# Rotating a matrix by 90 degrees: filling both PSUM tiles row tile by row tile in the first output of a macro tile

## The chip, the cores and the metric

The kernel runs on one core of one Trainium2 chip. Times are device microseconds (us) of one execution. A profile comes from one of these executions; its span runs from the first to the last instruction and is about 2 us shorter than the time (1266.0 us of 1267.77 in the kernel before).

In this kernel SP issues the loads, DVE reverses rows, PE transposes blocks of 128 by 128 into tiles in PSUM (`pt` in the profile's lines), ACT copies from there into an output buffer and issues the stores, and 16 DMA engines move the data. A DMA share of 1.0 means that all 16 are busy. PE's clock is given as a share of its full speed; the records show 1.00 and 0.50 (in the kernel before, 0.50 from 1214 to 1216.5 us and 1.00 from 1221.5 to 1222.5 us), and a mean in between where it turns.

## The reference

```python
def setup_inputs():
    return {
        "x": np.random.randn(8192, 8192).astype(np.float32),
        "k": 1,
    }

def reference(x, k):
    return np.rot90(x, k)
```

A counter-clockwise turn by 90 degrees is a reversal of each row followed by a transpose. The matrix has 268 MB, and each byte is read once and written once.

## The kernel before

The matrix is cut into macro tiles of 1024 rows by 4096 columns. Each has eight row tiles of 128 rows, and each row tile is one load of 2 MB. There are 15 full macro tiles. The sixteenth is cut into two half-height ones of four row tiles each, and both are loaded before either is put out.

```python
def load(r0, rt, c0):                       # rt = 8, or 4 for a half-height macro tile
    for t in range(rt):
        a = a_pool.tile([P, W], dt, tag="a")                  # 2 buffers
        nc.sync.dma_start(out=a[:], in_=x[r0 + t*P : r0 + (t+1)*P, c0 : c0 + W])
        for j in range(W // CH):
            ar = r_pool.tile([P, CH // P, P], dt, tag="ar")   # 68 buffers
            nc.vector.tensor_copy(out=ar[:], in_= ... [:, :, ::-1])   # reversal
            chunks[t, j] = ar
# ... cut: the first loads borrow o_pool's buffers

def store(r0, rt, c0, chunks, end):
    # full height: PW = 2, G = 4.  half height: PW = 4, G = 8
    for i, g0 in enumerate(range(0, W // P, G)):              # one output = one store of 2 MB
        ot = o_pool.tile([P, F], dt, tag="o")                 # 2 buffers (cut: at the end a_pool's too)
        for h in range(0, G, PW):                             # two PSUM tiles for each output
            pt = psum_pool.tile([P, FP], mybir.dt.float32, tag="ps")   # 2 buffers
            for w in range(PW):
                for t in range(rt):
                    nc.tensor.transpose(ps[...], chunks[t, ...], ident)   # 16 for each PSUM tile
            nc.scalar.copy(o[:, G - PW - h : G - h, :], ps)
            # after the second copy: the store, issued on ACT's queue
            ...
            nc.scalar.dma_start(out=dst, in_=...)
# ... cut
for m in most:
    store(*m, load(*m), False)
c1 = load(*before_last)
c2 = load(*last)
store(*before_last, c1, True)
store(*last, c2, True)
```

A tile framework adds all waits, and a scheduler orders the instructions of each engine. The order in the source goes tile by tile: an output's first PSUM tile gets all its 16 transposes, two for each row tile in a full-height macro tile, before the second gets any. So when the last row tile of a macro tile arrives, only 7 of the first output's 32 transposes are done.

Of the kernel before, what the change touches and what calls it, by code (L numbers as in the profile page):

```python
# [2 lines left out]

# [5 lines left out]

P = 128  # L10




R = 1024
RT = R // P
LAST = [4, 4]
W = 4096
CH = 512
F = 4096  # L20
FP = 2048


def whole_reads(nc):






    for fn in nc.m.functions:
        for block in fn.blocks:
            for n, ins in enumerate(block.instructions):
                if not isinstance(ins, mybir.InstDMACopy):
                    continue
                src = ins.ins[0]
                ap = [list(d) for d in src.ap]
                if len(ap) == 3 and ap[2][0] == 1 and ap[1][0] == ap[2][1]:
                    ap = [ap[0], [1, 1], [1, ap[1][1] * ap[2][1]]]
                    block.instructions[n] = copy.replace(  # L40
                        ins,
                        ins=[copy.replace(src, ap=ap)],
                        ant_dge_precooked=False,
                    )


def macro_tiles(N, M):

    tiles = [(r0, RT, c0) for r0 in range(0, N, R) for c0 in range(0, M, W)]
    r0, _, c0 = tiles.pop()  # L50
    for n in LAST:
        tiles.append((r0, n, c0))
        r0 += n * P
    return tiles


@with_exitstack
def kernel(
    ctx: ExitStack,
    tc: tile.TileContext,  # L60
    x: bass.AP,
    k: bass.AP,
    out: bass.AP,
):
    nc = tc.nc
    assert k == 1, f"only k=1 supported, got {k}"
    nc.at_finalize(whole_reads)

    N, M = x.shape
    dt = x.dtype  # L70

    consts = ctx.enter_context(tc.tile_pool(name="consts", bufs=1))
    ident = consts.tile([P, P], dt)
    make_identity(nc, ident)

    a_pool = ctx.enter_context(tc.tile_pool(name="a_pool", bufs=2))
    r_pool = ctx.enter_context(tc.tile_pool(name="r_pool", bufs=68))
    o_pool = ctx.enter_context(tc.tile_pool(name="o_pool", bufs=2))
    psum_pool = ctx.enter_context(
        tc.tile_pool(name="psum", bufs=2, space=bass.MemoryType.PSUM)  # L80
    )

    loads = 0

    def load(r0, rt, c0):





        nonlocal loads
        chunks = {}
        for t in range(rt):


            if loads < RT and loads % 4 >= 2:
                a = o_pool.tile([P, W], dt, tag="o")
            else:
                a = a_pool.tile([P, W], dt, tag="a")
            loads += 1  # L100
            nc.sync.dma_start(
                out=a[:], in_=x[r0 + t * P : r0 + (t + 1) * P, c0 : c0 + W]
            )
            for j in range(W // CH):
                ar = r_pool.tile([P, CH // P, P], dt, tag="ar")
                nc.vector.tensor_copy(  # L106
                    out=ar[:],
                    in_=a[:, j * CH : (j + 1) * CH].rearrange(
                        "r (b m) -> r b m", m=P
                    )[:, :, ::-1],  # L110
                )
                chunks[t, j] = ar
        return chunks

    def store(r0, rt, c0, chunks, end):





        rows = rt * P
        PW = 1
        while 2 * PW * rows <= FP:
            PW *= 2
        G = PW
        while 2 * G * rows <= F:
            G *= 2
        for i, g0 in enumerate(range(0, W // P, G)):
            if end and i % 2 == 0:
                ot = a_pool.tile([P, F], dt, tag="a")  # L130
            else:
                ot = o_pool.tile([P, F], dt, tag="o")
            o = ot[:, : G * rows].rearrange("m (g f) -> m g f", g=G)

            S = PW if end and r0 + rows == N and g0 + G == W // P else G
            for h in range(0, G, PW):
                pt = psum_pool.tile([P, FP], mybir.dt.float32, tag="ps")
                ps = pt[:, : PW * rows].rearrange("m (g f) -> m g f", g=PW)
                for w in range(PW):
                    g = g0 + h + w  # L140
                    for t in range(rt):
                        nc.tensor.transpose(  # L142
                            ps[:, PW - 1 - w, t * P : (t + 1) * P],
                            chunks[t, g * P // CH][:, g % (CH // P), :],
                            ident,
                        )
                nc.scalar.copy(o[:, G - PW - h : G - h, :], ps)  # L147

                done = h + PW
                if done % S == 0:  # L150
                    top = M - c0 - (g0 + done) * P
                    dst = out[top : top + S * P, r0 : r0 + rows].rearrange(
                        "(g m) f -> m g f", g=S
                    )
                    nc.scalar.dma_start(  # L155
                        out=dst, in_=o[:, G - done : G - done + S, :]
                    )

    tiles = macro_tiles(N, M)
    *most, before_last, last = tiles  # L160
# [9 lines that stand above are left out]
# [1 line left out]
_INS = ['x', 'k']  # L171
_OUTS = [((8192, 8192), 'float32')]

_NUMBERS = {'k': 1}


# [26 lines left out]
```

## Time and profile before

| What | Value |
| --- | --- |
| time, median of 3 runs | 1267.77 us (1267.59 to 1268.42) |
| span of the profiled run | 1266.0 us |
| PE, DVE, ACT busy | 55%, 28%, 37% |
| DMA, mean rate over the span | 425 GB/s |
| idle time of ACT before its copies | 742.6 us, of which 729.5 us wait for a store to free its buffer |
| one output on ACT | two copies of 1.87 us and the issue of the store (0.55 us) |

The way to read this is from the last row upward. ACT waits for stores most of the time (729.5 us), PE waits for ACT (465.9 us), and DVE waits for loads (811.4 us). These waits lead back, for the most part, to the DMA, whose share is 1.01, at 429 GB/s, from 70 to 980 us.

### The profile page before, as it was taken

The page shows a single profiled execution, that of the slowest core. Times are in us where ns is not written, and L with a number is a line of the kernel's source. Part 1 is how long each engine was busy: PE and PEld are TensorE (multiplying, and loading weights), DVE is VectorE, ACT ScalarE, POOL GpSimd, SP SyncE. Part 2 cuts the span into 40 slices and gives each one's busy share as a digit, 9 for nine tenths or more (in the row PEclk, how much of TensorE's full clock was granted, in tenths as well). Part 3 has the DMA queues.
Part 4 walks back from the last instruction along what each step waited for, and adds up shares of the span by engine and source line. Part 5 has one row for each costly group of instructions (what it writes and reads, how often), then busy time and mean ns, then how long its engine had stood idle before and what let it go on. Part 6 is the DMA issues. An engine that isn't in the chain of part 4 may idle for free.

```text
span 1266.0 us, 10386 instructions
## 1 busy us (share of the span) xinstructions
PE 700.4 (55%) x4096; PEld 660.8 (52%) x4096; DVE 354.9 (28%) x1024; ACT 467.3 (37%) x257; POOL 0.7 (0%) x6
## 2 busy tenths in 40 slices
PE   1456455665655555555556546565464665656573
PEld 0355455554545455554555445464464654556573
DVE  4422322232222322233222322233222332223210
ACT  0333334333433334333433334333433334333364
POOL 0000000000000000000000000000000000000000
PEclk9986777777678777787777877778777667777687
DMA  9999999999999999999999999999999999999998
GB/s 398 416 431 429 429 428 429 430 427 430 427 429 429 429 429 430 428 429 428 430 428 428 429 429 427 427 429 426 430 429 427 414 428 430 426 427 428 428 393 370
DMA packets 37057, 537.55 MB, mean 425 GB/s; under 512 B 4112, under 2 KB 4112, under 8 KB 4112
## 3 DMA queue, kind: packets, MB, share of 16 engines
q10 hardware_dynamic: 18576, 268.44, 50.0%
q1 hardware_dynamic: 18432, 268.44, 49.9%
q8 instruction: 32, 0.52, 0.2%
q14 instruction: 17, 0.14, 0.0%
HBM read 268.44 MB, written 268.44 MB: 424 GB/s over the span
## 4 chain that ended last, share of the span: by engine, by line
DMA 78%; ACT 19%; issue 1%; DVE 1%; ACTq 0%; PE 0%; DVEq 0%
DMA out_dram<-ot 74%; ACT ot L147 19%; DMA a<-in_x_dram 3%; DVE ar L106 1%; ACTq L155 0%; PE pt L142 0%; ACTq L147 0%; DVEq L106 0%
## 5 line engine op out<-in xcount | busy, mean ns | idle before, releaser
L142 PE MATMUL pt<-ident,ar 128*128 128x128 f32 x4096 | 700.4, 350 | 548.3 <-ACT ot L147 465.9
L142 PEld LDWEIGHTS pt<-ident,ar 128*128 128x128 f32 x4096 | 660.8, 187 | 587.7 <-ACT ot L147 496.4
L147 ACT COPY ot<-pt 128x2048 f32<-128x2048 f32 x256 | 466.0, 1869 | 742.6 <-DMA out_dram<-ot 729.5
L106 DVE COPY ar<-a 128x512 f32<-128x512 f32 x1024 | 354.9, 420 | 865.8 <-DMA a<-in_x_dram 811.4
L147 ACT ACT_TABLE_LOAD x1 | 1.3, 1283 | 41.1 <-DVE ar L106 41.1
masks.py:199 POOL TENSOR_SCALAR_AFFINE_SELECT ident<-ident 128x128 f32<-128x128 f32 x1 | 0.3, 294 | 0.1
masks.py:197 POOL MEMSET ident<- 128x128 f32 x1 | 0.2, 205 | 0.3 <-POOLq L184 0.3
L184 POOL MEMSET const-bfloat16-1.0<- 128x1 bf16 x1 | 0.1, 102 | 0.0
L184 POOL MEMSET const-uint8-127<- 128x1 uint8 x1 | 0.1, 102 | 0.0
L184 POOL MEMSET const-float32-0.0<- 128x1 f32 x1 | 0.1, 99 | 0.2 <-issue 0.2
L184 POOL MEMSET const-float32-1.0<- 128x1 f32 x1 | 0.1, 99 | 0.0
## 6 DMA issues: line engine op xcount, KB each, us to landing
a<-in_x_dram SPq DMA_DIRECT2D x128, 2048.0 KB, 16.8
out_dram<-ot ACTq DMA_DIRECT2D x127, 2048.0 KB, 15.9
out_dram<-ot ACTq DMA_DIRECT2D x2, 1024.0 KB, 13.7
```

The lines of the kernel that those rows point to most:

```text
L106: nc.vector.tensor_copy(out=ar[:], in_=a[:, j * CH : (j + 1) * CH].rearrange("r (b m) -> r b m", m=P)[:, :, ::-1],)
L142: nc.tensor.transpose(ps[:, PW - 1 - w, t * P : (t + 1) * P], chunks[t, g * P // CH][:, g % (CH // P), :], ident,)
L147: nc.scalar.copy(o[:, G - PW - h : G - h, :], ps)
L184: nc = _bacc.Bacc("TRN2", target_bir_lowering=False, num_devices=1)
```

## The change

The intent is to shorten what has to follow the arrival of a macro tile's last row tile. For the first output, both PSUM tiles are taken at once, and the transposes go by row tile over both of them: 28 of the 32 can be done before the last row tile has come, and four remain instead of 25.

```diff
+            ps = {}
+
+            def transposes(t, ws):
+                for w in ws:
+                    g = g0 + w
+                    nc.tensor.transpose(
+                        ps[w // PW][:, PW - 1 - w % PW, t * P : (t + 1) * P],
+                        chunks[t, g * P // CH][:, g % (CH // P), :],
+                        ident,
+                    )
+
+            def psum_tile(h):
+                pt = psum_pool.tile([P, FP], mybir.dt.float32, tag="ps")
+                ps[h] = pt[:, : PW * rows].rearrange("m (g f) -> m g f", g=PW)
+
+            if i == 0 and (rt == RT or r0 + rows < N):
+                for h in range(G // PW):
+                    psum_tile(h)
+                for t in range(rt):
+                    transposes(t, range(G))
             for h in range(0, G, PW):
-                pt = psum_pool.tile([P, FP], mybir.dt.float32, tag="ps")
-                ps = pt[:, : PW * rows].rearrange("m (g f) -> m g f", g=PW)
-                for w in range(PW):
-                    ... (16 transposes into this tile)
-                nc.scalar.copy(o[:, G - PW - h : G - h, :], ps)
+                if h // PW not in ps:
+                    psum_tile(h // PW)
+                    for w in range(h, h + PW):
+                        for t in range(rt):
+                            transposes(t, [w])
+                nc.scalar.copy(o[:, G - PW - h : G - h, :], ps[h // PW])
```

The condition takes in the 15 full macro tiles and the first of the two half-height ones.

More of the change, by code (lines that the diff above doesn't have):

```diff
@@ L135, in store @@
             S = PW if end and r0 + rows == N and g0 + G == W // P else G
-            for h in range(0, G, PW):
-                pt = psum_pool.tile([P, FP], mybir.dt.float32, tag="ps")
-                ps = pt[:, : PW * rows].rearrange("m (g f) -> m g f", g=PW)
-                for w in range(PW):
-                    g = g0 + h + w
-                    for t in range(rt):
-                        nc.tensor.transpose(
-                            ps[:, PW - 1 - w, t * P : (t + 1) * P],
-                            chunks[t, g * P // CH][:, g % (CH // P), :],
-                            ident,
-                        )
-                nc.scalar.copy(o[:, G - PW - h : G - h, :], ps)
+            ps = {}
[15 more added lines that the diff above has]
+                    transposes(t, range(G))
+            for h in range(0, G, PW):
+                if h // PW not in ps:
[4 more added lines that the diff above has]
+                nc.scalar.copy(o[:, G - PW - h : G - h, :], ps[h // PW])
                 done = h + PW
```

## The prediction

> **What bounds the kernel now.** I read the page's busy row and its slices first, then the chain that ended last, then a table of stretches, then the timeline at one macro tile boundary, then the chain through the end.
>
> ```profile
> PE 700.4 (55%) x4096; PEld 660.8 (52%) x4096; DVE 354.9 (28%) x1024; ACT 467.3 (37%) x257; POOL 0.7 (0%) x6
> ...
> DMA  9999999999999999999999999999999999999998
> ...
> DMA 78%; ACT 19%; issue 1%; DVE 1%; ACTq 0%; PE 0%; DVEq 0%
> ```
>
> No compute engine is over 55% busy, and the DMA row is full in 39 of 40 slices. In the chain that ended last, PE has 0%. The 19% of ACT in that chain lies, in the steady state, beside other transfers: a store's landing releases the two copies into its buffer, while another store and two loads are still under way. So the question is not how long the chain is but when the 16 DMA engines run dry. The table of stretches answers it; its last three columns are the granted PE clock, the DMA share and GB/s, and its first count is PE's instructions.
>
> ```profile
> 4.00:50.00 46.00, 11.14 (x46) 7.98 (x47) 24.16 (x70) 5.02 (x3) 0.00 (x0) 1.00 1.00 428
> 50.00:70.00 20.00, 11.38 (x85) 10.62 (x82) 5.79 (x18) 7.28 (x4) 0.00 (x0) 0.83 1.01 409
> 70.00:980.00 910.00, 507.69 (x2951) 480.63 (x2951) 255.65 (x738) 338.32 (x186) 0.00 (x0) 0.75 1.01 429
> ...
> 1214.00:1216.50 2.50, 2.50 (x13) 2.50 (x13) 0.00 (x0) 1.43 (x1) 0.00 (x0) 0.50 0.27 111
> 1216.50:1221.50 5.00, 4.78 (x43) 4.50 (x42) 2.78 (x8) 3.69 (x3) 0.00 (x0) 0.98 0.99 419
> 1221.50:1222.50 1.00, 1.00 (x11) 1.00 (x10) 0.00 (x0) 1.00 (x1) 0.00 (x0) 1.00 0.70 295
> ```
>
> From 4 us to 1214 us the DMA share is 1.0 throughout, at 428 to 429 GB/s but for small dips (409 at 50 to 70 us). The engines run dry in three places only: the first 4 us, 1214 to 1216.5 us (share 0.27), and the end. The second is where the loads are over and only stores remain, just as the first half-height macro tile starts to be put out. Of everything the change touches, only that place lies next to an idle DMA.
>
> [...] PE idles 3 to 6 us between outputs, the granted clock is 0.50 at many restarts, and 32 transposes take 3.7 us (warm) to 6.6 us (cold).
> [...] 32 of them took 3.74 us with the clock at 1.00 and 16 took 3.40 us at 0.50, that is 0.11 us and 0.21 us apiece. I use the trace's figures.
>
> **The change part by part.** Counts are unchanged: 4096 transposes, 1024 reversals, 256 copies, and the built programs have the same order on ACT, DVE and SP. Only the order on PE differs, in the first output of 16 of the 17 macro tiles (15 full ones and the first of two half-height ones), 32 transposes each. One copy (ACT) empties one PSUM tile (16 transposes), two copies make one store.
>
> *(a) The 14 inner boundaries.* The timeline of one:
>
> ```profile
> 583.63 1.36 PEld L142 LDWEIGHTS pt<-ident,ar 128*128 128x128 f32 x7 [4.13 <-ACT ot L147]
> ...
> 588.31 4.50 PEld L142 LDWEIGHTS pt<-ident,ar 128*128 128x128 f32 x25 [3.32 <-DVE ar L106]
> 588.31 4.74 PE L142 MATMUL pt<-ident,ar 128*128 128x128 f32 x25 [2.92 <-DVE ar L106]
> 591.49 3.63 ACT L147 COPY ot<-pt 128x2048 f32<-128x2048 f32 x2 [6.14 <-DMA out_dram<-ot]
> ```
>
> PE does 7, waits for the last row tile at 588.31, does 25 and ends at 593.05. ACT starts at 591.49, because a store's landing let it, and needs the second PSUM tile at 591.49 + 1.87 = 593.36: PE is 0.3 us early. After the change 28 transposes come before the last row tile's four. In the built program the order is 8 into the first PSUM tile, 8 into the second once its copy has ended (about 585.4), then four for each later row tile. At 0.21 us each they end near 585.4 + 24 x 0.21 = 590.4. So both tiles are full by about 590.5, 1 us before the first copy and 3 us before the second. What is removed is ACT's small stall at the boundaries where PE was late: the timeline shows four (0.27, 0.95, 0.57 and 0.50 us, 2.3 us in all). But the DMA share is 1.0 there, so a store issued half a microsecond sooner only queues longer. I count 0 for this part.
>
> *(b) The first macro tile.* Its last row tile is ready at 43.6 us, and the first copy starts at 45.83 after 9 more transposes into its tile; it will be 2 (0.4 us instead of about 1.9). So the first two stores go out some 1.5 us sooner, at about 48.1 and 52.7 instead of 49.65 and 54.16. In that time loads fill the DMA engines, so this mostly swaps loads for stores. Only the dip to 409 GB/s between 50 and 70 us (20 us x 20/429 = 0.9 us lost) could shrink. I count -0.3 us, a guess within 0 to -0.9.
>
> *(c) The half-height macro tile at the end.* All its rows were converted long before, so it has no last row tile to wait for. The chain through this place:
>
> ```profile
> 1195.80 15.92 DMA out_dram<-ot
> ...
> 1211.80 1.88 ACT ot L147
> 1213.67 0.04 issue
> 1213.72 3.40 PE pt L142 x16
> 1217.12 0.02 issue
> 1217.14 3.66 ACT ot L147 x2
> 1220.80 0.02 issue
> 1220.82 0.55 ACTq L155
> ```
>
> Here PE is on the path. It gets a free PSUM tile at 1213.67, fills it with 16 transposes by 1217.12, and only then can ACT copy. After the change the same 32 transposes are dealt out over both tiles, and the built program lets the first copy go after the 28th instead of the 16th. The whole 32 took 5.13 us here (the clock turns at about 1216.6), so the 28th ends at about 5.13 - 4 x 0.11 = 4.7 us after 1213.72, against 3.40: the first copy is 1.3 us later, and the second follows without a wait, as the second tile is then full. The store of 1220.82 goes out at about 1222.1. The one before it is off the engines by about 1221.5, so they idle 1.3 us longer. Nothing makes up for it: a 2 MB store lasts 5.0 us at 418 GB/s and ACT makes one each 4.31 us, so from 1222 on the engines drain eight stores back to back. The end moves by the whole +1.3 us.
>
> **Sum:** 1267.8 + 0 - 0.3 + 1.3 = 1268.8 us.
>
> **The rivals.** *Earlier stores shorten the whole run.* If the 1.5 us of (b) were kept and the 2.3 us of ACT stalls of (a) were on the path, the time would fall to about 1267.8 - 3.8 + 1.3 = 1265.3 us. For it speaks that ACT waits on PE 12.1 us in all; against it, that ACT waits 729.5 us for store buffers and that the share is 1.0 where it would have to gain.
> *The phase at the end shifts.* If stores run a little ahead of loads, the last load has more left when the loads end and fills the hole at 1214 us. The most it could win is that hole, 2.5 x 0.73 = 1.8 us, for about 1267 us. Against it: the offset between DVE's and ACT's starts is 3.6 to 3.7 us from 80 us to 1160 us, so an early lead does not seem to be kept.
> *A cold PE becomes the bound.* [...] At 0.21 us, 25 transposes last 5.3 us; in the changed order only 4 of them come after the data, so at the boundaries this does no harm, and at the end it would make the 28th 28 x 0.21 = 5.9 us, +2.5 instead of +1.3: 1270 us.
>
> **Range and chances.** The three runs before span 0.8 us. The tail term is +1.3 (up to +2.5), the start 0 to -0.9, the phase up to -1.8. That gives 1266.4 to 1270.4. Two per cent is 25 us, ten times any of these terms: all DMA idle time outside the first 4 us and the last 4 us is some 2.1 us (2.5 x 0.73 + 1.0 x 0.3). So within 2% has 0.98.
>
> **What would show it.** Right: the DMA share stays 1.0 from 4 to 1214 us; PE's groups at boundaries become small ones with four after the last row tile; ACT's waits on PE at the boundaries vanish; at the end ACT's wait for PE before the half-height tile's first copy grows from 1.71 us to about 3 us and the store after it is issued 1.3 us later against the end of the loads. Wrong: a time under 1266.4, above all with a hole at the end of the loads that has closed, or a rate above 429 GB/s in the middle; or ACT still late at the boundaries because PE is held by the second PSUM tile's copy.

Its sum came to 1268.8 us. The 0 of part (a) stands as the estimate from the measured share of 1.0, to be tested by the runs; part (b), a guess within bounds, part (c), and the 0.11 and 0.21 us for one transpose are reckoned from the trace of the kernel before.

## The result, and the profile after

The changed kernel is correct and took 1270.16 us, median of six runs (1269.55 to 1270.63). The kernel before took 1268.09 us in the same rounds (1267.59 to 1269.21). The ratio is 1.0016, with a 95% interval of 1.0003 to 1.0028: about 2 us slower. Here and below, a difference in us is one of the mean times of the two kernels in the same rounds, so it is not quite that of the medians.

The page of the changed kernel: the busy row, the DMA's row of slices, and the chain that ended last, by engine.

```profile
PE 723.0 (57%) x4096; PEld 685.8 (54%) x4096; DVE 355.2 (28%) x1024; ACT 466.7 (37%) x257; POOL 0.7 (0%) x6
...
DMA  9999999999999999999999999999999999999989
...
DMA 77%; ACT 19%; PE 1%; issue 1%; ACTq 0%; DVE 0%; SPq 0%
```

Nothing but PE's busy time has moved: counts are equal, and ACT and DVE are as busy as before. PE now has 1% of the last chain instead of 0%, and the DMA's weak slice is the one before the last instead of the last. The table of stretches of the changed kernel says where (the first pair of numbers is the stretch and its length, the last three columns are PE's clock, the DMA share and GB/s):

```profile
50.00:70.00 20.00, 12.86 (x81) 12.38 (x79) 6.53 (x19) 7.38 (x4) 0.00 (x0) 0.74 1.01 425
70.00:1212.00 1142.00, 665.53 (x3715) 634.36 (x3712) 321.95 (x928) 421.66 (x232) 0.00 (x0) 0.75 1.01 428
1215.00:1218.00 3.00, 3.00 (x14) 2.80 (x15) 2.21 (x7) 1.67 (x1) 0.00 (x0) 0.50 0.32 137
1218.00:1223.00 5.00, 3.48 (x25) 3.25 (x24) 0.57 (x2) 2.43 (x2) 0.00 (x0) 0.83 0.92 390
1223.00:1225.50 2.50, 2.50 (x25) 2.46 (x24) 0.00 (x0) 1.83 (x2) 0.00 (x0) 1.00 0.12 52
```

The start is a little fuller than before (425 GB/s instead of 409), and the long middle is the same (428 GB/s, share 1.01). The hole where the loads end is still there (0.32 over 3 us). Behind the one store that follows it there is now a second hole, 2.5 us at a share of 0.12, where the kernel before had 1 us at 0.70. The store that ends it was issued by ACT at 1224.24 us, when the DMA had been idle since 1223 us (share 0.00), and these two stretches show the DMA idle for 1.0 us more and busy right after. Counted from the end of the 0.55 us that the issue took, it is 0.45 us:

```profile
1224.24:1225.24 1.00, 1.00 (x11) 0.98 (x10) 0.00 (x0) 0.36 (x1) 0.00 (x0) 1.00 0.00 0
1225.24:1225.49 0.25, 0.25 (x5) 0.25 (x3) 0.00 (x0) 0.25 (x1) 0.00 (x0) 1.00 1.08 459
```

*At the inner boundaries* the change does what it was made for. The timeline of the changed kernel at the macro tile boundary that the prediction shows of before (start, length, engine, and in brackets the idle time before it and what ended it):

```profile
584.77 1.57 PEld L143 LDWEIGHTS pt<-ident,ar 128*128 128x128 f32 x8 [4.87 <-ACT ot L164]
...
585.35 2.77 DVE L106 COPY ar<-a 128x512 f32<-128x512 f32 x8 [7.01 <-DMA a<-in_x_dram]
...
586.54 3.38 PEld L143 LDWEIGHTS pt<-ident,ar 128*128 128x128 f32 x24 [0.20 <-ACT ot L164]
...
592.61 3.64 ACT L164 COPY ot<-pt 128x2048 f32<-128x2048 f32 x2 [6.13 <-DMA out_dram<-ot]
```

PE works 8 and then 24 transposes in one go, with 0.20 us between them while it waits for the second PSUM tile, and is done at about 590.2, 2.4 us before ACT's buffer is free. Before, it ended at 593.05, after ACT's first copy had begun. The waits between 100 and 1205 us, first of the kernel before and then of the changed one (total us, number, longest):

```profile
ACT ot L147 <- DMA out_dram<-ot: 697.4, 113, 6.9
...
ACT ot L147 <- PE pt L142: 2.3, 4, 0.9
```

```profile
ACT ot L164 <- DMA out_dram<-ot: 700.3, 113, 7.1
```

The 2.3 us that ACT waited for PE have gone, and the changed kernel has no row for that wait at all. ACT's wait for stores has grown by 2.9 us instead.

*At the start* the first store is issued earlier. ACT and its queue between 45 and 50 us, before and after:

```profile
45.83 3.79 ACT L147 COPY ot<-pt 128x2048 f32<-128x2048 f32 x2 [3.42 <-PE pt L142]
49.65 0.65 ACTq L155 DMA_DIRECT2D out_dram<-ot  x1
```

```profile
44.52 3.63 ACT L164 COPY ot<-pt 128x2048 f32<-128x2048 f32 x2 [1.99 <-PE pt L143]
48.18 0.65 ACTq L172 DMA_DIRECT2D out_dram<-ot  x1
```

That is 1.47 us sooner (49.65 - 48.18). In this profile the second output doesn't keep the lead: its store goes out at 54.93 us instead of 54.16, because PE was slower at it. Between 48 and 52 us it did 20 transposes, where the kernel before did 32, after a break of 1.53 us that the old order, busy with the first output until then, did not have. Other profiles differ: in the six that have the new order in the first macro tile, the second store goes out between 53.24 us (e3_first_tile) and 54.93, and in those with the old order there between 53.85 and 54.32.

*At the end* the change lengthens the path. The chain of the changed kernel that answers to the one shown in the prediction:

```profile
1213.04 1.87 ACT ot L164
1214.91 0.04 issue
1214.95 5.59 PE pt L143 x28
1220.55 0.02 issue
1220.57 0.46 ACT ot L164
1221.03 1.30 issue
1222.33 1.88 ACT ot L164
1224.22 0.02 issue
1224.24 0.55 ACTq L172
```

Where the kernel before had 16 transposes in 3.40 us between two copies, this one has 28 in 5.59 us. ACT's wait, before and after, is in the brackets of these two lines:

```profile
1217.14 3.65 ACT L147 COPY ot<-pt 128x2048 f32<-128x2048 f32 x2 [1.71 <-PE pt L142]
```

```profile
1220.57 3.63 ACT L164 COPY ot<-pt 128x2048 f32<-128x2048 f32 x2 [3.90 <-PE pt L143]
```

From the start of the last full macro tile's last copies (1211.80 and 1213.04) to the end of the half-height macro tile's second copy (1217.14 + 3.65 = 1220.79, and 1224.20) it was 8.99 us before and 11.16 us after, 2.2 us more. I use this distance below, as it can be read in every run.

### The profile page after: what moved, and what is told of

Read it like the earlier page. It is cut to its first block, busy times and chain, and to the rows that moved or that the text cites. A ratio compares the mean times of both kernels' runs of the same rounds, so it can differ in the third digit from the quotient of the medians.

```text
span 1268.7 us, 10387 instructions
## 1 busy us (share of the span) xinstructions
PE 723.0 (57%) x4096; PEld 685.8 (54%) x4096; DVE 355.2 (28%) x1024; ACT 466.7 (37%) x257; POOL 0.7 (0%) x6
## 4 chain that ended last, share of the span: by engine, by line
DMA 77%; ACT 19%; PE 1%; issue 1%; ACTq 0%; DVE 0%; SPq 0%
DMA out_dram<-ot 74%; ACT ot L164 19%; DMA a<-in_x_dram 3%; PE pt L143 1%; ACTq L172 0%; DVE ar L106 0%; SPq L101 0%; ACTq L164 0%
## 5 line engine op out<-in xcount | busy, mean ns | idle before, releaser
L143 PE MATMUL pt<-ident,ar 128*128 128x128 f32 x4096 | 723.0, 359 | 529.1 <-ACT ot L164 493.1
L143 PEld LDWEIGHTS pt<-ident,ar 128*128 128x128 f32 x4096 | 685.8, 192 | 566.0 <-ACT ot L164 527.0
```

Of the source, the lines that this page charges most:

```text
L143: nc.tensor.transpose(ps[w // PW][:, PW - 1 - w % PW, t * P : (t + 1) * P], chunks[t, g * P // CH][:, g % (CH // P), :], ident,)
```

## The experiments

All kernels gave the reference's result. Those of one round ran on one chip and share the runs of the kernel before. "Distance" is the one just defined.

| Run | Order changed where | Median, us | Before in its rounds | Mean against before, us | Ratio (95%) | Distance, us |
| --- | --- | --- | --- | --- | --- | --- |
| changed kernel | full and half-height | 1270.16 | 1268.09 | +2.0 | 1.0016 (1.0003 to 1.0028) | 11.16 |
| e1_full_tiles | full only | 1268.87 | 1268.04 | +0.8 | 1.0006 (0.9994 to 1.0019) | 9.81 |
| e2_half_tile | half-height only | 1269.19 | 1268.04 | +1.0 | 1.0007 (0.9993 to 1.0021) | 10.47 |
| e3_first_tile | first tile only | 1267.67 | 1268.04 | -0.1 | 0.9999 (0.9987 to 1.0012) | 9.14 |
| e4_inner_tiles | 14 inner ones only | 1268.20 | 1268.04 | +0.1 | 1.0000 (0.9988 to 1.0013) | 9.20 |
| g1_before_again | nowhere | 1267.76 | 1268.59 | -0.1 | 0.9999 (0.9986 to 1.0011) | 9.21 |
| g2_after_again | full and half-height | 1269.64 | 1268.59 | +1.4 | 1.0012 (0.9999 to 1.0026) | 11.13 |
| g3_full_again | full only | 1269.47 | 1268.59 | +1.1 | 1.0008 (0.9995 to 1.0020) | 10.32 |
| f1_fill | nowhere, other end | 1273.01 | 1268.59 | +4.4 | 1.0034 (1.0022 to 1.0047) | |
| h1_halves | nowhere, stores halved | 1267.77 | 1268.11 | -0.2 | 0.9998 (0.9984 to 1.0011) | 9.91 |
| h2_halves_after | full and half-height, stores halved | 1269.45 | 1268.11 | +1.6 | 1.0013 (1.0000 to 1.0025) | 10.82 |
| i1_all32 | half-height, all 32 first | 1269.90 | 1268.11 | +1.8 | 1.0014 (1.0002 to 1.0027) | 10.96 |
| g4_inner_again | 14 inner ones only | 1268.15 | 1268.25 | -0.2 | 0.9999 (0.9985 to 1.0012) | 8.94 |

### The parts of the change alone

My theory is that of the prediction: the half-height macro tile costs time, the inner boundaries do nothing, and the start helps a little. The main rivals were that the inner boundaries or the start move the whole stream, or that the time comes from PE's clock. The condition of the changed kernel is narrowed in four ways.

The 15 full macro tiles only:

```diff
-            if i == 0 and (rt == RT or r0 + rows < N):
+            if i == 0 and rt == RT:
```

> The change in the 15 full macro tiles only; the half-height tile keeps the old order. Theory (the cost is the 28th transpose that the half-height tile's first copy waits for): ACT's wait for PE there is back at about 1.7 us and the time is that of the kernel before within 0.5 us. Rival (the new offset between loads and stores, seen in the trace from 62 us on, costs time in the long middle): the time stays 1.2 us or more above the kernel before.

The half-height macro tile only:

```diff
-            if i == 0 and (rt == RT or r0 + rows < N):
+            if i == 0 and rt < RT and r0 + rows < N:
```

> The change in the first half-height macro tile only. Theory: all of the cost, +1.3 us if PE's clock turns early there and +2.2 us if it stays at half over the 28 transposes; ACT's wait for PE before that copy is 3.0 to 3.9 us in place of 1.7. Rival (cost from the offset between loads and stores): under +1 us.

The first macro tile only:

```diff
-            if i == 0 and (rt == RT or r0 + rows < N):
+            if i == 0 and r0 == 0 and c0 == 0:
```

> The change in the first macro tile only. Theory: 0 to -0.9 us; the first store goes out at about 48.2 us in place of 49.65. Rival (offset): ACT's starts then lie some 7 us after DVE's in the middle, in place of 3.7, and the time is about 1.2 us above the kernel before.

The 14 inner boundaries only:

```diff
-            if i == 0 and (rt == RT or r0 + rows < N):
+            if i == 0 and rt == RT and r0 + c0 > 0:
```

> The change in the 14 inner boundaries only. Theory: no effect, within 0.5 us of the kernel before, as the DMA engines are full there, though ACT's stalls of 0.3 to 0.95 us on PE at these boundaries vanish. Rival (stalls on the path): up to 2.3 us faster.

*Measured.* The half-height macro tile alone costs 1.0 us, and its trace shows the longer wait (timeline of e2_half_tile):

```profile
1219.36 3.64 ACT L164 COPY ot<-pt 128x2048 f32<-128x2048 f32 x2 [3.20 <-PE pt L143]
```

ACT waits 3.20 us instead of 1.71, and the distance is 10.47 us. The wait is the expected one; the time is less than the expected +1.3 to +2.2 us and, at +0.96, even within the rival's bound, so by itself it doesn't tell the two apart. The full tiles alone fell between the expectations as well: +0.8 us, where the theory said within 0.5 and the rival 1.2 or more, and ACT's wait at the half-height tile was 2.00 us rather than 1.7. The inner boundaries alone have lost ACT's wait for PE just as the whole change has (waits of e4_inner_tiles between 100 and 1205 us; again there is no row of ACT for PE):

```profile
ACT ot L164 <- DMA out_dram<-ot: 700.8, 113, 7.1
```

Its time is that of the kernel before, to 0.1 us. A gain of 2.3 us lies outside its interval (-1.5 to +1.6 us), so these waits were not on the path. The first macro tile alone issues its first store early too (its first copy starts at 44.08 us) and moves 427 GB/s from 50 to 70 us instead of 409, and gains 0.1 us, which can't be told from nothing. Its offset between DVE's and ACT's starts near 670 us is 4.66 us, not the 7 us that the rival expected.

*What follows.* The order of size is as predicted, but these runs don't close the sum. No interval of the four excludes zero. Also, e3 and e4 are the two halves of e1 and show nothing, whereas e1 shows +0.8 us. So the next runs repeat it.

### The same kernels again, and a filled hole

g1_before_again is the kernel before, g2_after_again the changed kernel and g3_full_again the kernel of e1_full_tiles, without any edit.

> The kernel before itself, as a null: 0 within 0.5 us, and a second trace of it. From the start of the copy that waits for the last store of the full tiles to the end of the span 54.2 us, as in the first trace, unless PE's clock turns later there.

> The changed kernel again, for a second trace and five more times. Theory (start -0.5 us, end +1.4 us, nothing between): +0.9 us. If the full tiles' part costs something of its own, as the run of that part alone leaves open (+0.8 us, interval -0.8 to +2.4): +2 us again, as first measured.

> The change in the full tiles only, again. Theory: -0.5 to 0 us (the first store goes out 1.5 us sooner, nothing else on the path). Rival (a cost of its own in the 15 full tiles): +0.8 us again, with the DMA share below 1.0 somewhere between 70 and 1200 us.

*Measured.* The kernel before against itself came out at 0.9999, so the comparison shows no bias, but its interval is 3.2 us wide. From the copy to the end of the span it took 53.7 us and not the 54.2 expected. The changed kernel was slower by 1.4 us, halfway between the theory (+0.9) and the cost in the full tiles (+2), and its second profile has a wait of 3.86 us and a distance of 11.13 us, nearly those of the first. Changing the full macro tiles alone gave +1.1 us, again with an interval across zero. That misses the theory (-0.5 to 0 us), and the rival's sign is missing too: the DMA share was 1.01 from 70 to 1200 us.

These traces also refute a sentence of the prediction: that the offset between DVE's and ACT's starts is kept at 3.6 to 3.7 us. The timelines near 670 us, of the kernel before and of the same kernel again:

```profile
666.39 2.77 DVE L106 COPY ar<-a 128x512 f32<-128x512 f32 x8 [7.03 <-DMA a<-in_x_dram]
...
670.07 3.64 ACT L147 COPY ot<-pt 128x2048 f32<-128x2048 f32 x2 [6.14 <-DMA out_dram<-ot]
```

```profile
665.43 2.77 DVE L106 COPY ar<-a 128x512 f32<-128x512 f32 x8 [7.04 <-DMA a<-in_x_dram]
...
670.44 3.64 ACT L147 COPY ot<-pt 128x2048 f32<-128x2048 f32 x2 [6.13 <-DMA out_dram<-ot]
```

The offset is 3.68 us in one and 5.01 us in the other, with the same program. In the two profiles of the changed kernel it is 7.26 and 4.74 us. So the offset changes from run to run; the prediction had read a habit of one trace as a property of the kernel. What the offset is worth at the end is taken up below, under the runs together.

The fourth kernel of this round tests whether the hole at the end of the loads (0.27 over 2.5 us in the kernel before) can be filled. It stores seven outputs of the last full macro tile, then loads all but one row tile of the half-height ones, stores the eighth output, and loads the last row tile behind it (cut: the hunks that let `load` and `store` take a part of a macro tile, and that choose the buffer):

```diff
+    c0 = load(*most[-1])
+    store(*most[-1], c0, False, range(7))
     c1 = load(*before_last)
-    c2 = load(*last)
-    store(*before_last, c1, True)
-    store(*last, c2, True)
+    c2 = load(*last, range(last[1] - 1))
+    store(*most[-1], c0, True, [7], 1)
+    c2 |= load(*last, [last[1] - 1])
+    store(*before_last, c1, True, odd=1)
+    store(*last, c2, True, odd=1)
```

> The kernel before, but the last output of the last full tile is put into a load buffer, ahead of the very last load, so that this store goes out some 6 us sooner and the last load later. Theory (what counts is when the DMA engines run dry at the end of the loads, 1.9 us in the kernel before): that hole closes, -1.5 to -1.9 us. Rival (the hole only moves to a later place): within 0.5 us.

*Measured.* My theory fell, and so did the rival's bound of 0.5 us: the time rose by 4.4 us. The stretches and the timeline of f1_fill:

```profile
1203.50:1206.00 2.50, 2.17 (x13) 2.17 (x14) 0.00 (x0) 2.05 (x2) 0.00 (x0) 0.68 0.33 138
1228.00:1231.00 3.00, 2.44 (x12) 2.44 (x13) 0.00 (x0) 2.27 (x2) 0.00 (x0) 0.50 0.03 11
```

```profile
1215.46 0.55 ACTq L157 DMA_DIRECT2D out_dram<-ot  x1
1226.64 3.63 ACT L149 COPY ot<-pt 128x2048 f32<-128x2048 f32 x2 [11.21 <-DVE ar L106]
```

The hole only moved: holding the last load back leaves 2.5 us at a share of 0.33 before it. Then ACT stands still for 11.21 us, as the next output goes into the buffer in which the last load had landed, and DVE had to reverse it first. A second hole of 3 us follows that wait (share 0.03). One wait was replaced by a longer one.

### Half stores, and more transposes ahead of the first copy

h1_halves takes the kernel before, and h2_halves_after the changed kernel, and both issue the three stores around the end of the loads in two halves, each after its own copy, so that the DMA gets work sooner:

```diff
             S = PW if end and r0 + rows == N and g0 + G == W // P else G
+            if (r0, c0) == (N - R, 0) and i >= 6 or (r0, c0) == (N - R, W) and i == 0:
+                S = PW
```

> The kernel before, with three stores (the last two of the full tiles and the first of the half-height tile) issued as two halves, each as soon as its own copy is done, 1.9 us sooner for the first half. Theory (the DMA engines running dry between 1210 and 1230 us, share 0.81 to 0.89 there, is what sets these few us): the share there rises towards 1.0 and the time falls by 1 to 1.9 us. Rival (the bytes or issues cost as much as they gain, as with the load buffer): within 0.5 us.

> The same three halved stores on the changed kernel. Theory: the hole that waiting for the 28th transpose leaves gets 1.9 us shorter as well, so the time falls by 2 to 3 us against the changed kernel, to about the kernel before or 1 us under it. Rival: still 1.5 us or more above the kernel before.

i1_all32 changes the half-height macro tile alone, and fills the second PSUM tile before the first, so that the first copy waits for all 32 transposes rather than 28:

```diff
-            if i == 0 and (rt == RT or r0 + rows < N):
-                for h in range(G // PW):
+            if i == 0 and rt < RT and r0 + rows < N:
+                for h in reversed(range(G // PW)):
                     psum_tile(h)
-                for t in range(rt):
-                    transposes(t, range(G))
+                    for w in range(h * PW, (h + 1) * PW):
+                        for t in range(rt):
+                            transposes(t, [w])
```

> Only the half-height tile's first output differs from the kernel before: its second PSUM tile is filled first, so the first copy waits for all 32 transposes in place of 16 (before) or 28 (the change). Theory (dose): ACT's wait for PE there is 3.4 to 4.4 us in place of 1.7, and the time is +1.5 to +2.3 us, more than the +1.0 of the change in that tile alone. Rival (not the wait, something else in that tile): no more than +1 us.

*Measured.* Halving the stores gave -0.2 us on the kernel before, and left +1.6 us on the changed one: both times the rival held, and my theory fell. The stretches of h1_halves show why:

```profile
1214.00:1216.00 2.00, 1.99 (x10) 1.99 (x11) 0.00 (x0) 1.73 (x1) 0.00 (x0) 0.50 0.72 303
1220.00:1221.00 1.00, 1.00 (x11) 1.00 (x10) 0.00 (x0) 0.86 (x1) 0.00 (x0) 1.00 0.32 131
1226.00:1228.00 2.00, 2.00 (x21) 1.96 (x20) 0.00 (x0) 1.33 (x2) 0.00 (x0) 1.00 0.58 229
```

The first hole has closed from 0.27 to 0.72, and two later ones have opened. I read this so: the same bytes were put out earlier, and PE and ACT, which feed the DMA there, had made nothing new in the meantime. That would also be why issuing sooner did not hide the half-height tile's delay; no run tests the reading by itself.

The timeline of i1_all32 shows the larger delay:

```profile
1219.38 3.63 ACT L165 COPY ot<-pt 128x2048 f32<-128x2048 f32 x2 [3.70 <-PE pt L143]
...
1224.65 1.87 ACT L165 COPY ot<-pt 128x2048 f32<-128x2048 f32 x1 [1.63 <-PE pt L143]
```

ACT waits 3.70 us for the first copy, and then 1.63 us more at the next output. PE had stood idle for 1.96 us before that output, and its mean clock was 0.57 from 1221.3 to 1224.6 us, against 1.00 in the same stretch of e2_half_tile, so in this profile the second wait is one for a halved clock. The time is +1.8 us, with an interval above zero. Against e2_half_tile, the same place with 28 instead of 32, the longer wait goes with the longer time (+1.0 and +1.8 us), as it should if PE is on the path there; how much of the step is the four transposes and how much the clock, one profile doesn't tell.

### The inner boundaries again

The kernel of e4_inner_tiles once more, without an edit, to see whether its zero holds.

> The change in the 14 inner boundaries only, again. The two runs of all full tiles gave some +0.9 us, but their parts gave -0.1 us (first tile) and +0.1 us (inner boundaries). If the parts' first figures were low by chance and the inner boundaries carry that cost: +0.5 to +1 us here. If they are free, as theory says: within 0.4 us of the kernel before, and the +0.9 us stays open.

*Measured.* -0.2 us, ratio 0.9999. It holds.

### The runs together

Every kernel in which the half-height macro tile's order is changed was slower: +2.0, +1.4, +1.0, +1.6 and +1.8 us. The five that change neither this part nor all full macro tiles, f1_fill apart (e3, e4, g1, g4 and h1), lie within 0.2 us of the kernel before. The distance agrees. In the eight profiles with the old order at the half-height macro tile its mean is 9.44 us (8.94 to 10.32). In the four with the new order (i1_all32 apart) it is 10.90 us (10.47 to 11.16). The two sets don't overlap, and the difference is 1.46 us. From the same first copy to the end of the span it is 54.3 us (53.7 to 54.9) with the old order and 55.3 us (54.8 to 55.7) with the new one, so about 1.0 us of the difference reaches the end.

The spread within a set goes with PE's clock. With the old order, its mean over 1210 to 1230 us is 0.91 in the five profiles with distances of 8.94 to 9.21 us and 0.83 in the three with 9.81 to 10.32 us; with the new one it is 0.91 in e2_half_tile (10.47 us) and 0.83 in the other three (10.82 to 11.16 us). PE does nothing but transposes here, and the clock turns full in the midst of them: in the kernel before, 14 ran in the 2.96 us at 0.50 after PE's restart at the half-height macro tile (1213.72 to 1216.68 us), about 0.21 us apiece, and the 32 from 1219.07 us on took 3.74 us at 1.00 (their weight loads 3.50 us), 0.11 to 0.12 us apiece. In the same kernel, the mean clock of 0.98 over 1216.5 to 1221.5 us says that it turned full 5 x 0.02 / 0.5 = 0.2 us into that stretch, at about 1216.7, which is 3.0 us after PE's restart at 1213.72. In the changed kernel, 0.83 over 1218 to 1223 us gives 1.7 us into it, at about 1219.7, 4.7 us after the restart at 1214.95. With the clock turning 1.7 us later, the 28 transposes took 5.59 us rather than the 4.7 us reckoned. In e2_half_tile they took 4.89 us. The old order shows it too: before the first and the second copy ACT waits for PE 2.00 and 0.44 us in e1_full_tiles and 2.00 and 0.96 us in g3_full_again (mean clock 0.83), against 1.71 and 0 us in the kernel before and 1.40 and 0.42 us in g1_before_again (0.91).

*What the distance leaves out* is when it begins. Its first copy waits for a store to land (6.21 us in the kernel before), and loads and stores share the DMA engines (there the two queues of 268 MB took 50.0% and 49.9% of the 16 engines' span). These lines show the last reversal of that stretch and the copy, in the kernel before and in the changed one:

```profile
1208.10 2.77 DVE L106 COPY ar<-a 128x512 f32<-128x512 f32 x8 [7.04 <-DMA a<-in_x_dram]
...
1211.80 3.63 ACT L147 COPY ot<-pt 128x2048 f32<-128x2048 f32 x2 [6.21 <-DMA out_dram<-ot]
```

```profile
1205.97 2.77 DVE L106 COPY ar<-a 128x512 f32<-128x512 f32 x8 [7.10 <-DMA a<-in_x_dram]
...
1213.04 3.64 ACT L164 COPY ot<-pt 128x2048 f32<-128x2048 f32 x2 [7.11 <-DMA out_dram<-ot]
```

The offset between the two starts is 3.70 us before and 7.07 us after: in the changed kernel's profile the loads are further ahead of the stores. Of the 2.7 us by which its span is longer, 1.24 lie before this copy and 1.46 after it. Two more profiles have such an offset, g3_full_again (7.36 us) and h2_halves_after (7.09); their copies start at 1213.32 and 1212.87 us. In the other ten (f1_fill apart) the offset is 3.7 to 6.1 us and the copy starts between 1211.44 and 1212.53. What this goes with can be seen where the order at the half-height tile is the old one: the four profiles with 3.7 us and whole stores have spans of 1265.6 to 1266.4 us, g3_full_again has 1268.2, to which its clock (mean 0.83 over 1210 to 1230 us, distance 10.32 us) also adds. And with the new order but 3.68 us, g2_after_again has 1267.1. So where loads and stores stand to each other at the end goes with about as many us as the 28th transpose. Three of the five profiles with the new order in all full tiles have the offset of 7 us and none of the eight others, but g2_after_again is the very program of the changed kernel. Whether the change brings this offset about or chance does, thirteen profiles don't settle.

No version tried here beats both kernels by more than the scatter.

## Why the prediction was right or wrong

**Total: right.** The time is within the range, and the class is the one given 0.98. It is 1.4 us above the point, and of that 0.3 us is the kernel before, which was at 1268.09 us in these rounds rather than 1267.77.

**(a) Inner boundaries, 0: right, within the scatter.** ACT's 2.3 us of waits went away, ACT waited for stores instead (700.3 us, after 697.4), and two studies of this part alone gave +0.1 and -0.2 us, with intervals that exclude a gain of 2.3 us but not one of 1 us.

**(b) Start, -0.3 us: mechanism right, gain not found.** The first store went out 1.47 us sooner, as reckoned, and the dip at 50 to 70 us shrank. Alone it gave -0.1 us, which can't be told from zero or from -0.3 with this scatter. The step "the second store too" isn't borne out: it went out 0.77 us later than before in the changed kernel's profile, and 0.92 us sooner in e3_first_tile's.

**(c) Half-height tile, +1.3 us: mechanism and size right, but not "the whole".** In the profiles with the new order the path is 1.46 us longer; about 1.0 us of that reaches the end of the span, and this part alone cost 1.0 us. The wait grew to 3.20 us (e2_half_tile) and 3.90 us (changed kernel), where "about 3 us" was predicted. The larger figure is the "cold PE" rival in part: in this profile the clock came on later (mean 0.83 over 1210 to 1230 us, against 0.91 in e2_half_tile). (The prediction read its 16 transposes in 3.40 us as at a clock of 0.50; the mean clock of that stretch is 0.57, as the clock had turned before the last of them. That changes little: 14 ran in the 2.96 us before it turned, about 0.21 us apiece.) That the end moves with this wait rests on the five kernels with the new order together, all slower and with longer distances, of which the first rounds of the changed kernel and i1_all32 have intervals clear of zero by themselves, h2_halves_after just touches it, and those of g2_after_again and e2_half_tile contain it.

**The step that failed is the sum, by a term that it set to 0: the phase at the end.** It took -0.3 us for all full macro tiles. Measured, the whole change costs 1.4 to 2.0 us against 1.0 us for the half-height tile, and the full tiles as a set gave +0.8 and +1.1 us. Yet the first tile and the inner ones, each alone, gave nothing, and the intervals of both full-tile runs contain zero. What the traces show in place of the 0 is the offset between loads and stores: the prediction took it as fixed at 3.6 to 3.7 us and left it out of the sum, except as a possible gain. In the changed kernel's profile it was 7.07 us at the end, and 1.24 of the 2.7 us of longer span had passed before the half-height tile's part began; g3_full_again shows such a loss without any change at that tile. The full-tile profiles also have two of the three longest distances of the old order (9.81 and 10.32 us), with the clock at a mean of 0.83 over 1210 to 1230 us in both, against 0.91 in the kernel before (in e1_full_tiles the 32 transposes there took 6.00 us, against 5.13), so the clock has added some of it. Whether the change causes this or chance is open. That the total still fell into the range is in part luck: the range has room above for a cold PE, none for a phase that costs time.

**The rivals.** "Earlier stores shorten the whole run" fell: the middle ran at the same 428 GB/s, and no part gave a gain. "The phase at the end shifts" was right that it shifts and wrong in the sign: it was not seen as a gain, and the hole at the end of the loads stayed (0.32 over 3 us). The argument against it was wrong too, as the offset isn't kept even between two runs of one kernel.

## What to carry to other kernels

Ask of a reordering where the DMA engines are idle, and price it there alone: 14 boundaries at which a wait really went away gave no gain that could be measured at a share of 1.01, and the clearest cost lay at the one place with an idle DMA (0.27 over 2.5 us before the change). Here the order made for data that arrive late cost time where they had long been there, because interleaving two buffers delays the first one (full after 28 transposes and 5.59 us, instead of 16 and 3.40); such a change should be conditional on the wait that it is made for. And where an effect is as small as the scatter between runs, let the length of a stretch in the trace speak beside the time, over several profiles, note also when the stretch begins, and repeat the kernel before against itself.
